# A hybrid diffusion layer on one core: later bank clearing, stepped head tails, earlier mLSTM decays, reordered output weights

## The chip, the cores and the metric

The kernel runs on one core of one Trainium2 chip. The metric is the device time of one execution in microseconds; lower is better. Three runs of the kernel before the change took 1374.45, 1374.62 and 1376.55 us, so its median is 1374.62 us. One further execution was taken with the hardware profiler; all rows of the trace below come from it.

The engines have short names in the profile: PE is TensorE (matrix products), PEld its weight loads, DVE is VectorE, ACT is ScalarE, POOL is GpSimd, and SP is the queue that issues nearly all DMAs. Every engine works its own queue strictly in order; between engines there are semaphores.

## The reference

One layer over 512 latent tokens (model width 1024) with 256 context tokens ahead of them, all in fp32:

```python
mod_x = (silu(c) @ w_ada + b_ada)            # six rows of 1024: shift, scale, gate, twice
hc = rms_norm(ctx, norm1_w) * (1 + mod_c[1]) + mod_c[0]
hx = rms_norm(x, norm1_w) * (1 + mod_x[1]) + mod_x[0]
_, states = token_mixer(hc, zero_states, False, ...)
x_mix, _ = token_mixer(hx, states, True, ...)
x = x + mod_x[2] * x_mix
hx = rms_norm(x, norm2_w) * (1 + mod_x[4]) + mod_x[3]
x = x + mod_x[5] * conv_ffn(hx, w_up, ffn_conv, w_down)   # 3x3 depthwise conv, silu gate, 2816 wide
return rms_norm(x, norm_out_w)
```

The token mixer has two branches, each run forward and backward over the tokens. The gated DeltaNet branch has 8 heads (keys and values 128 wide), the mLSTM branch has 4 (keys 128, values 256). Both are linear recurrences computed chunk by chunk: inside a chunk with a decay matrix, between chunks with a state. Each head's output is normalised and multiplied by a gate; the branches are projected back, merged by sigmoid gates and projected by `w_out`.

## The kernel before, in words

Tokens are taken in 6 chunks of 128 (2 of context, 4 latent). Large products are made in three passes of split operands (`mm3`, lines 117 to 122): a weight is cast to a high part on ScalarE (line 108) and its low part is a subtraction on VectorE or GpSimd (line 109). A raw weight lies in one of two to three raw buffers, its parts in as many split buffers; a load waits for a free one.

The stages follow each other: `streams` (norm, first modulation), `mixers` (12 heads), `merge` (branch projections and gates), `tail` (output projection, second norm, FFN, last norm).

In `mixers`, a loop over `s` runs the scan of head `s`: 0 to 7 are `gdn_scan`, 8 to 11 are `ml_scan`. A scan is a generator that yields after each short step. `drive` (line 1181) pulls it and, after each step, pulls side work at listed steps and a share of bulk work:

- the tail of the head before (`gdn_tail`, `ml_tail`), at steps 1, 4 and 6 (`TAIL`): square sums, a power on GpSimd, scaled copies out of PSUM, transposes;
- `merges(s + 1)` at steps 3, 4, 6, 8, 10, 12 and 13 (`MERGE`): it assembles the triangular inverses of the next head, and makes `qs`, the queries times a decay row that it loads by DMA;
- `ada_late`: the last four modulation rows by GpSimd products of `w_ada` tiles, some steps per scan from `s = 6` on; `ada_sum` adds them up in a PSUM tile `pad` on TensorE;
- as bulk, the preparation of head `s + 2` (`gdn_prep`, `ml_prep`): projections, keys, decay matrices `E` (loaded as rows by `decay_rows`, made by `weights`).

A scan adds its outputs into one PSUM bank `po`, of which there is one. `gdn_scan` clears it by a product with zeros (line 956) before its first step, and adds with `out` (line 961) from its third chunk step on. The bank is free when the tail of the head before has copied it out (line 1023).

The order in each queue is not the order of the lines. A planner lists all instructions, gives earlier lines priority, estimates durations, and issues on each engine what it takes to be ready. `queue_after(later, earlier)` ties an instruction behind another in this plan; `follow(ins, key)` ties it behind the latest anchor of that key: "t" for TensorE, "v" for VectorE, "s" for ScalarE, "d" for loads, "w" for casts, "p" for GpSimd. The result is a fixed queue per engine; on the chip an instruction whose input is late holds all behind it.

In `tail`, weights of `w_out` come in pairs of row blocks (`w_pair`, 512 KB each), four for each half of the output columns. The loads are serial (each tied behind the one before): the first half, a modulation row, `x` in four pieces, the second half from a separate pool, two modulation rows, then four weight tiles of `w_up` with a quarter of the filter rows `frow` behind each. The filter rows are transposed on TensorE into `fw` between the second half's products.

## Time and profile before

| | |
|---|---|
| median of 3 runs | 1374.62 us (1374.45 to 1376.55) |
| profiled execution, its time | 1377.58 us |
| its span, first to last instruction | 1375.8 us |
| mean granted TensorE clock | 0.983 |
| TensorE busy | 1310.2 us, 95% |
| VectorE busy | 890.2 us, 65% |
| ScalarE busy | 586.7 us, 43% |
| GpSimd busy | 541.4 us, 39% |
| DMA | 141.86 MB, mean 103 GB/s |

Each row of a timeline gives the start in us from the span's start, the duration in us, the engine, the line, the operation, `output<-inputs` by tile names, the shapes, and how many instructions the row holds. In square brackets stands how long the engine was idle just before, and which instruction or DMA ended that. A row of the view of waits gives who waited for whom, the sum in us, how often, and the longest. Matmuls are pipelined, so a busy TensorE is not TensorE at its peak: a matmul under a lowered clock counts as busy too. In time, the clearings of heads 1 to 7 run at about 238, 302, 359, 419, 475, 537 and 589 us, the mLSTM scans fill about 650 to 826, the merge 826 to 943, the output projection and second norm 943 to 1013, the FFN the rest.

### The profile page before, as it was taken

How to read it: one execution, taken by the hardware profiler on the slowest of the kernel's cores; microseconds unless marked ns; L12 is line 12 of the kernel's file. 1: busy time of each engine (PE TensorE's matmuls, PEld its weight loads, DVE VectorE, ACT ScalarE, POOL GpSimd, SP SyncE). 2: the span in 40 equal slices, each digit the busy share in tenths (PEclk: the TensorE clock that was granted, in tenths of full speed). 3: DMA queues.
4: the chain of work that ended last, by engine and by line, in shares of the span. 5: the costliest groups of instructions: out<-in, count | busy, mean ns of one | idle time of the engine just before them, and what ended most of it. 6: DMA issues, size and time to landing. Idle time of an engine off the chain costs nothing. (4 is left out here: it accounts for less than half of the span.)

```text
span 1375.8 us, 24216 instructions
## 1 busy us (share of the span) xinstructions
PE 1310.2 (95%) x9454; PEld 1103.0 (80%) x9454; DVE 890.2 (65%) x1809; ACT 586.7 (43%) x1283; POOL 541.4 (39%) x679
## 2 busy tenths in 40 slices
PE   6978999989899899999999999999899999999997
PEld 5867788878788788888888978888698888888876
DVE  5776686947568583524656466443769797997843
ACT  5555574645555554323333445221433333333322
POOL 4324222031231317475775670000246555455542
PEclk9989999999999999999999999999999999999999
DMA  9433233232232335343444432434623233333221
GB/s 284 123 103 81 76 90 106 67 76 76 53 90 62 81 69 139 99 123 92 129 120 112 116 100 69 138 107 168 175 77 107 92 92 92 105 95 90 94 92 62
DMA packets 233281, 141.86 MB, mean 103 GB/s; under 512 B 33025, under 2 KB 215566, under 8 KB 233166
## 3 DMA queue, kind: packets, MB, share of 16 engines
q1 hardware_dynamic: 231006, 140.09, 36.6%
q8 instruction: 74, 1.21, 0.4%
q10 hardware_dynamic: 2160, 0.23, 0.1%
q14 instruction: 41, 0.34, 0.1%
HBM read 134.47 MB, written 5.82 MB: 102 GB/s over the span
## 5 line engine op out<-in xcount | busy, mean ns | idle before, releaser
L1571 DVE SCALAR_TENSOR_TENSOR y<-pu,fw,y 128x441 f32<-128x441 f32 (+2 forms) x352 | 230.0, 691 | 43.1 <-ACT y L1562 37.2
L294 POOL TENSOR_TENSOR aw<-aw,sc 128x512 f32<-128x512 f32 x64 | 69.5, 1087 | 47.1 <-DMA aw<-in_w_ada_dram 47.1
L143 POOL TENSOR_TENSOR rs<-pw_t,mhalf 128x1 f32<-128x1 f32 x14 | 8.2, 583 | 167.5 <-DVE pw_t L142 167.5
L295 POOL TENSOR_TENSOR aw<-aw 128x256 f32<-128x256 f32 x64 | 54.4, 851 | 3.3
L143 POOL TENSOR_TENSOR kh<-pw_t,phalf 128x6 f32<-128x6 f32 x8 | 12.0, 1502 | 108.4 <-DVE pw_t L142 64.3
L884 POOL TENSOR_TENSOR qs<-qs,qT 128x512 f32<-128x512 f32 x16 | 25.0, 1565 | 69.3 <-DMA qs<-gd 58.6
L832 POOL MEMSET gx<- 96x16 f32 x8 | 1.0, 123 | 121.2 <-DMA gx<-scr 121.2
L986 ACT ACTIVATE v<-p,sc 128x128 f32<-128x128 f32 x80 | 25.5, 371 | 36.5 <-PE p L978 36.1
L974 DVE SCALAR_TENSOR_TENSOR X<-p,colA,vt 128x128 f32<-128x128 f32 x80 | 24.1, 339 | 25.1 <-PE p L970 24.8
L839 POOL TENSOR_TENSOR gx<-gx,iv_t 96x14 f32<-96x14 f32 (+6 forms) x112 | 36.6, 327 | 8.4
L1325 DVE SCALAR_TENSOR_TENSOR x<-x,py 128x512 f32<-128x512 f32 x16 | 11.0, 687 | 43.8 <-PE py L120 43.8
L1501 POOL TENSOR_TENSOR al<-y,ah 128x512 fp32r<-128x512 f32 x22 | 28.5, 1296 | 26.4 <-ACT ah L1500 26.4
L1562 ACT ACTIVATE y<-pu,fw 128x512 f32<-128x512 f32 x44 | 29.9, 682 | 17.7 <-PE pu L120 16.3
L990 PEld LDWEIGHTS p<-v,kt 128*128 128x128 f32 x160 | 22.6, 195 | 17.9 <-ACT v L986 16.7
L1133 DVE SCALAR_TENSOR_TENSOR C<-C,ge,mpc 128x257 f32<-128x257 f32 x32 | 15.3, 479 | 32.4 <-PE mpc L1129 32.0
L997 DVE SCALAR_TENSOR_TENSOR S<-S,ge,p 128x128 f32<-128x128 f32 x64 | 19.3, 340 | 26.2 <-PE p L990 25.8
L837 POOL TENSOR_TENSOR iv_t<-gx 96x14 f32<-96x14 f32 (+6 forms) x112 | 33.0, 295 | 8.0
L647 ACT ACTIVATE cv_t<-cv_y 128x512 f32<-128x512 f32 (+1 forms) x40 | 21.8, 545 | 33.6 <-DVE cv_y L646 32.7
L698 DVE SCALAR_TENSOR_TENSOR Eg<-Eg,colA,mask 128x128 f32<-128x128 f32 x96 | 31.5, 398 | 1.7 <-DMA Eg<-gd 1.7
L990 PE MATMUL p<-v,kt 128*128 128x128 f32 x160 | 27.9, 296 | 3.0 <-ACT v L986 3.0
L1003 ACT ACTIVATE v<-p,sc 128x128 f32<-128x128 f32 x64 | 22.9, 376 | 16.8 <-PE p L990 13.9
L1500 ACT CAST ah<-y 128x512 fp32r<-128x512 f32 x22 | 13.6, 619 | 38.0 <-DVE y L1499 37.8
(1222 smaller groups left out, 4593.4 us busy)
## 6 DMA issues: line engine op xcount, KB each, us to landing
aw<-in_w_ada_dram SPq DMA_DIRECT2D x64, 256.0 KB
uw<-in_w_ada_dram SPq DMA_DIRECT2D x16, 512.0 KB
Eg<-gd SPq DMA_DIRECT2D x16, 384.0 KB
qs<-gd SPq DMA_DIRECT2D x16, 256.0 KB
xn<-in_x_dram SPq DMA_DIRECT2D x4, 512.0 KB
Em<-r1d SPq DMA_DIRECT2D x8, 256.0 KB
mwo_0r<-in_w_in_dram SPq DMA_DIRECT2D x4, 512.0 KB
mwo_1r<-in_w_in_dram SPq DMA_DIRECT2D x4, 512.0 KB
```

The source lines that it names most:

```text
L294: self.follow(eng.tensor_tensor(w, w, self.sc[:, 4 * (j % 2) : 4 * (j % 2) + 4, 0:1].broadcast_to([P, 4, P]), ALU.mult))
L295: eng.tensor_tensor(w[:, 0:2, :], w[:, 0:2, :], w[:, 2:4, :], ALU.add)
L698: self.follow(nc.vector.scalar_tensor_tensor(E[:, c, :], E[:, c, :], self.colA[:, c, d, row : row + 1], self.mask[d], ALU.add, ALU.min), "v")
L837: eng.tensor_tensor(t, Bi[:, 0:j, j : j + 1].broadcast_to([8 * NB, j, n]), Bi[:, j : j + 1, j + 1 :].broadcast_to([8 * NB, j, n]), ALU.mult)
L839: g = eng.tensor_tensor(Bi[:, 0:j, j + 1 :], Bi[:, 0:j, j + 1 :], t, ALU.add)
L884: nc.gpsimd.tensor_tensor(x, x, qT, ALU.mult)
L974: self.anchor["v"] = nc.vector.scalar_tensor_tensor(X[d], p1[:, d, :], self.colA[:, c, 2 + d, h : h + 1], vt[:, c, :], ALU.mult, ALU.subtract)
L986: self.anchor["s"] = nc.scalar.activation(v3[d], p2[:, d, :], AF.Copy, scale=sc[d][:, 2 + j, c : c + 1])
L990: g = nc.tensor.matmul(p3[:, d, :], kt[:, c, :], v3[d], start=True, stop=True)
L1501: nc.gpsimd.tensor_tensor(al[:, j, :], ys[0], ah[:, j, :].bitcast(F32), ALU.subtract)
L1562: nc.scalar.activation(y, ps, AF.Copy, scale=tap(0, 0))
L1571: g = nc.vector.scalar_tensor_tensor(o, u3[:, r0 + dy : r1 + dy, c0 + dx : c1 + dx], tap(dy, dx), o, ALU.mult, ALU.add)
```

## The change

- The clearing of `po` moves from the start of a scan into `out`, just ahead of the first adding product, tied behind the scan's latest TensorE instruction.
- In `gdn_tail` the first seven heads yield between the power and the scaled copies, so the copies come at step 4 in place of step 1, tied behind ScalarE's latest scan instruction. The last head keeps its order.
- `qs` moves two stages later in `merges` (from the fourth stage to the sixth), and its multiplication on GpSimd is tied behind the latest power (`lastp`), that of a tail or of a head's key norm.
- Each tail's power becomes an anchor "q", behind which the products of `ada_late` are tied.
- In `ml_prep` the decay rows' loads come ahead of the key projection, and `weights` ahead of the output gate.
- The filter rows are loaded by one DMA at the start of `merge` and transposed there, into a tile `fw` that lives from there on.
- In `tail` the loads are reordered: all four pairs of the first half, two of the second, a modulation row and the first piece of `x`, the other two pairs, the rest of `x`, then two modulation rows; the fourth pair of the first half uses the separate pool, whose split buffers become five. In serial stretches, casts and subtractions are tied in order as well, and the FFN's second half becomes such a stretch.

```diff
--- before.py
+++ after.py
@@ -105,8 +105,12 @@
         lo = pool.tile(shape, F32R, tag="wlo", name=name + "l")
-        self.follow(nc.scalar.copy(hi, raw), "w")
+        c = nc.scalar.copy(hi, raw)
+        self.follow(c, "w")
         g = self.sub_eng.tensor_tensor(lo, raw, hi.bitcast(F32), ALU.subtract)
+        if self.serial:
+            self.follow(g, "l")
+            self.anchor["w"], self.anchor["l"] = c, g
         if self.late and self.sub_eng is nc.gpsimd:
@@ -140,7 +144,7 @@
         nc.vector.scalar_tensor_tensor(t, x, scale, (self.eps if bias else self.nil)[:, 0:n], ALU.mult, ALU.add)
-        nc.gpsimd.tensor_tensor(out, t, e[:, 0:n], ALU.pow)
+        return nc.gpsimd.tensor_tensor(out, t, e[:, 0:n], ALU.pow)
 
@@ -291,7 +295,9 @@
             nxt = load(j + 1) if j < 63 else None
-            self.follow(eng.tensor_tensor(w, w, self.sc[:, 4 * (j % 2) : 4 * (j % 2) + 4, 0:1].broadcast_to([P, 4, P]), ALU.mult))
+            g = eng.tensor_tensor(w, w, self.sc[:, 4 * (j % 2) : 4 * (j % 2) + 4, 0:1].broadcast_to([P, 4, P]), ALU.mult)
+            self.follow(g)
+            self.follow(g, "q")
             eng.tensor_tensor(w[:, 0:2, :], w[:, 0:2, :], w[:, 2:4, :], ALU.add)
@@ -733,7 +739,7 @@
         kh = small.tile([P, NCH], F32, tag="kh", name=f"kh{h}")
-        self.rpow(kh, ssk, 0.25, 0.0, self.phalf)
+        self.lastp = self.rpow(kh, ssk, 0.25, 0.0, self.phalf)
         yield 0.65
@@ -876,14 +882,6 @@
         yield
-
-        qs = []
-        for d in range(2):
-            x = hold.tile([P, NT], F32, tag="qs", name=f"qs{h}_{d}", bufs=4)
-            nc.sync.dma_start(x, self.gd[1, h, d : d + 1, NCTX:].broadcast_to([P, NT]))
-            nc.gpsimd.tensor_tensor(x, x, qT, ALU.mult)
-            qs.append(x)
-        self.qs[h] = qs
         DD = [(Bt[d], Dm_[:, d]) for d in range(2)]
@@ -915,6 +913,14 @@
         yield
+
+        qs = []
+        for d in range(2):
+            x = hold.tile([P, NT], F32, tag="qs", name=f"qs{h}_{d}", bufs=4)
+            nc.sync.dma_start(x, self.gd[1, h, d : d + 1, NCTX:].broadcast_to([P, NT]))
+            self.queue_after(nc.gpsimd.tensor_tensor(x, x, qT, ALU.mult), self.lastp)
+            qs.append(x)
+        self.qs[h] = qs
 
@@ -949,16 +955,16 @@
         qs = self.qs[h]
-        po = self.pt([P, XC, P], "po", f"po{h}")
-        self.po[h] = po
         S = [None, None]
         self.left = 4 * XC
-        nc.tensor.matmul(po, self.zero, self.zero.unsqueeze(1).broadcast_to([P, XC, P]), start=True, stop=False)
         order = [list(range(NCH)), list(range(CC - 1, -1, -1)) + list(range(NCH - 1, CC - 1, -1))]
...
         def out(x, a, b):
+            if self.left == 4 * XC:
+                self.po[h] = self.pt([P, XC, P], "po", f"po{h}")
+                self.follow(nc.tensor.matmul(self.po[h], self.zero, self.zero.unsqueeze(1).broadcast_to([P, XC, P]), start=True, stop=False))
             self.left -= 1
-            nc.tensor.matmul(po[:, x, :], a, b, start=False, stop=self.left == 0)
+            nc.tensor.matmul(self.po[h][:, x, :], a, b, start=False, stop=self.left == 0)
 
@@ -1017,12 +1023,15 @@
         nc.vector.scalar_tensor_tensor(f, ss, 1.0 / P, ssq, ALU.mult, ALU.add)
-        nc.gpsimd.tensor_tensor(f, f, self.mhalf[:, 0:XC], ALU.pow)
+        self.anchor["q"] = self.lastp = nc.gpsimd.tensor_tensor(f, f, self.mhalf[:, 0:XC], ALU.pow)
+        if h < GH - 1:
+            yield 0.0
         o = self.hold.tile([P, XC, P], F32, tag="o", name=f"o{h}", bufs=2)
         for c in range(XC):
-            nc.scalar.activation(o[:, c, :], po[:, c, :], AF.Copy, scale=f[:, c : c + 1])
+            self.follow(nc.scalar.activation(o[:, c, :], po[:, c, :], AF.Copy, scale=f[:, c : c + 1]), "s" if h < GH - 1 else None)
         yield 0.0
-        yield 0.0
+        if h == GH - 1:
+            yield 0.0
         ps = self.pt([P, 512], "prep", f"pot{h}")
@@ -1046,6 +1055,7 @@
         wk = self.w_cols(w, O_MK + P * h, f"mwk{h}")
+        E = [self.decay_rows(d, 8 + h, list(range(CC, NCH)), f"m{h}_{d}") for d in range(2)]
         kT = hold.tile([P, NALL], F32, tag="kT", name=f"mkT{h}", bufs=3)
@@ -1056,7 +1066,8 @@
         nc.scalar.activation(qT, p, AF.Copy, scale=P ** -0.5)
-        E = [self.decay_rows(d, 8 + h, list(range(CC, NCH)), f"m{h}_{d}") for d in range(2)]
+        for d in range(2):
+            self.weights(E[d], d, 8 + h, range(CC, NCH))
         og = []
@@ -1075,7 +1086,6 @@
         for d in range(2):
-            self.weights(E[d], d, 8 + h, range(CC, NCH))
             a = hold.tile([P, XC, P], F32, tag=f"at{d}", name=f"mp{h}_{d}", bufs=3)
@@ -1160,7 +1170,7 @@
         f = small.tile([P, XC], F32, tag="fo", name=f"mfo{h}")
-        self.rpow(f, ss, 1.0 / MDV, EPS, self.mhalf)
+        self.anchor["q"] = self.rpow(f, ss, 1.0 / MDV, EPS, self.mhalf)
         yield 0.0
@@ -1304,6 +1314,9 @@
                 pass
+            frow = self.flat(I["ffn_conv"]).rearrange("(c r p) -> r c p", r=99, p=P)
+            fr = self.hold.tile([99, 4, P], F32, tag="aw", name="frow", bufs=3)
+            nc.sync.dma_start(fr, frow)
             free = [self.slots[:, j, :] for j in range(self.nkept, 8)]
@@ -1325,6 +1338,8 @@
                 nc.vector.tensor_tensor(t[0], t[0], t[1], ALU.add)
+                if n < 4:
+                    self.cols_of(self.fw[:, 99 * n : 99 * n + 99], fr[:, n, :], 99)
                 nc.scalar.copy(self.mh[:, n, :], t[0])
@@ -1348,7 +1363,7 @@
             self.ps = es.enter_context(tc.tile_pool(name="ps", bufs=1, space=PSUM))
-            mg_es, l1 = ExitStack(), ExitStack()
+            mg_es, fw_es, l1 = ExitStack(), ExitStack(), ExitStack()
             with ExitStack() as e1:
@@ -1370,11 +1385,13 @@
                 self.dump("oTm", self.oTm)
+                self.fw = fw_es.enter_context(tc.tile_pool(name="fwp", bufs=1, side="right")).tile([P, 9 * 44], F32, tag="fw", name="fw")
                 self.mgt = mgt = mg_es.enter_context(tc.tile_pool(name="mgt", bufs=1, side="right"))
...
             self.tail(mg_es)
+            fw_es.close()
             l1.close()
@@ -1391,33 +1408,29 @@
             nw = lp.tile([P, D], F32, tag="nw", name="nw")
-            self.fw = lp.tile([P, 9 * 44], F32, tag="fw", name="fw")
             h2 = tuple(lp.tile([P, KC, NT], F32R, tag=f"h2{i}", name=f"h2{i}") for i in range(2))
...
                 m2, B2, A2 = rows = [ad1.tile([P, D], F32, tag=f"mr{i}", name=f"mr{i}") for i in range(3)]
-                x = (e2.enter_context(tc.tile_pool(name="wraw3", bufs=2)), e2.enter_context(tc.tile_pool(name="wsp3", bufs=4)))
+                x = (e2.enter_context(tc.tile_pool(name="wraw3", bufs=2)), e2.enter_context(tc.tile_pool(name="wsp3", bufs=5)))
                 w = I["w_out"][0]
...
                 self.wi, self.serial, self.anchor = 3, True, {}
-                wt = [self.w_pair(w, 0, b0) for b0 in range(0, KC, 2)]
+                wt = [self.w_pair(w, 0, 2 * i, x if i == 3 else None) for i in range(4)]
+                w1 = [self.w_pair(w, 1, 2 * i, x) for i in range(2)]
+                self.mod_row(0, m2)
+                self.load(x1[:, 0, :], I["x"][0, :P, :])
+                w1 += [self.w_pair(w, 1, 4, x), self.w_pair(w, 1, 6, x)]
+                for c in range(1, XC):
+                    self.load(x1[:, c, :], I["x"][0, c * P : c * P + P, :])
+                self.mod_row(2, A2)
+                self.mod_row(1, B2)
                 for b0 in range(0, KC, 2):
...
                         self.tok_mm(ps[c], wt[b0 // 2], self.mh, self.ml, b0, c, KC)
-                self.mod_row(0, m2)
-                for c in range(XC):
-                    self.load(x1[:, c, :], I["x"][0, c * P : c * P + P, :])
-                wt = [self.w_pair(w, 1, b0, x) for b0 in range(0, KC, 2)]
-                self.mod_row(2, A2)
-                self.mod_row(1, B2)
-                wu = []
-                frow = self.flat(I["ffn_conv"]).rearrange("(r p) -> r p", p=P)
-                fr = []
-                for b in (0, NFF, 1, NFF + 1):
-                    wu.append(self.w_cols(I["w_up"][0], P * b, f"wu{b}"))
-                    fr.append(ad1.tile([99, P], F32, tag="frow", name=f"frow{len(fr)}", bufs=4))
-                    self.load(fr[-1], frow[99 * len(fr) - 99 : 99 * len(fr), :])
+                self.wi = 3
+                wu = [self.w_cols(I["w_up"][0], P * b, f"wu{b}") for b in (0, NFF, 1, NFF + 1)]
                 self.serial = False
@@ -1431,8 +1444,7 @@
                     for i in range(4):
-                        self.tok_mm(p, wt[i], self.mh, self.ml, 2 * i, c, KC)
-                    self.cols_of(self.fw[:, 99 * c : 99 * c + 99], fr[c], 99, self.bank(5, f"ps_fw{c}"))
+                        self.tok_mm(p, w1[i], self.mh, self.ml, 2 * i, c, KC)
                     residual(c, 1, p)
@@ -1522,6 +1534,7 @@
             last = NFF - 6
+            self.serial = True
             for b0 in range(0, last, 2):
```

## The prediction

> **What bounds the kernel now.** I read the page first, then TensorE's waits by line, then the granted clock in short stretches, and last the engines' timelines around the longest waits. The first line of the page's part 1 says where the time is:
>
> ```profile
> PE 1310.2 (95%) x9454; PEld 1103.0 (80%) x9454; DVE 890.2 (65%) x1809; ACT 586.7 (43%) x1283; POOL 541.4 (39%) x679
> ```
>
> TensorE (PE) is busy for 95% of the span, and the change adds and removes no matmul. So it can only earn what TensorE loses to waiting, and it earns that one for one as long as no other engine takes its place. The view of waits, TensorE alone (us in total, times, longest), has these rows for the places that the change touches; the row of `mp` stands for comparison:
>
> ```profile
> PE po L956 <- ACT o L1023: 11.2, 4, 3.3
> ...
> PE p L990 <- ACT v L986: 3.0, 5, 0.6
> ...
> PE pv L119 <- ACT va L1099: 2.5, 1, 2.5
> PE mpqk L1075 <- DVE mkt L1071: 2.4, 1, 2.4
> ...
> PE mp L1137 <- ACT mn L1141: 2.2, 2, 1.6
> ...
> PE pt L1464 <- DVE h L1468: 2.1, 1, 2.1
> PE ps_fw L216 <- DMA frow<-in_ffn_conv_dram: 2.0, 2, 1.8
> ...
> PE pd L119 <- POOL wt_8l L109: 1.3, 1, 1.3
> ...
> PE po L119 <- DVE rs_t L1426: 0.7, 1, 0.7
> ```
>
> The largest single wait of the kernel is the clearing of a scan's bank (L956), which waits for the copies out of that bank (L1023). The touched rows add up to 11.2 + 3.0 + 2.5 + 2.4 + 2.1 + 2.0 + 1.3 + 0.7 = 25.2 us.
>
> A wait costs more than its own length here. The view of stretches (length, busy time of PE, PEld, DVE, ACT, POOL, then the granted TensorE clock, DMA share, GB/s) right behind five of these waits, with one undisturbed stretch between them:
>
> ```profile
> 302.00:307.00 5.00, 4.39 (x14) 3.48 (x14) 1.46 (x4) 3.53 (x8) 0.00 (x0) 0.66 0.00 0
> 360.50:364.50 4.00, 4.00 (x13) 3.27 (x14) 1.40 (x4) 2.80 (x7) 0.00 (x0) 0.57 0.02 4
> 476.50:480.50 4.00, 4.00 (x13) 3.28 (x14) 1.46 (x5) 2.86 (x7) 0.00 (x0) 0.57 0.00 0
> 480.50:530.00 49.50, 49.50 (x603) 42.57 (x602) 33.68 (x85) 27.22 (x84) 12.80 (x37) 1.00 0.35 80
> 633.00:638.00 5.00, 5.00 (x33) 5.00 (x32) 3.33 (x7) 0.52 (x2) 0.07 (x1) 0.66 0.53 152
> 995.50:999.50 4.00, 3.88 (x19) 3.32 (x19) 3.48 (x5) 2.16 (x4) 2.42 (x3) 0.57 0.01 2
> ```
>
> In each the clock falls for a few microseconds; the loss is 5 x (1 - 0.66) = 1.7 us, or 4 x (1 - 0.57) = 1.7 us. The reader is to see that a wait of 2 to 3 us is followed by 1.7 us more, lost in matmuls that look busy.
>
> Now the boundary between two scans, around 352 to 367 us: the timelines of POOL, VectorE (DVE), ScalarE (ACT) and TensorE in this order.
>
> ```profile
> 355.16 2.02 POOL L884 TENSOR_TENSOR qs<-qs,qT 128x512 f32<-128x512 f32 x1 [4.38 <-DMA qs<-gd]
> 357.14 1.01 POOL L1020 TENSOR_TENSOR fo<-fo,mhalf 128x4 f32<-128x4 f32 x1
> ```
>
> ```profile
> 351.83 0.16 DVE L1019 SCALAR_TENSOR_TENSOR fo<-sso,ssq 128x4 f32<-128x4 f32 x1 [1.50 <-ACT junk L1017]
> ```
>
> ```profile
> 358.18 1.14 ACT L1023 ACTIVATE o<-po,fo 128x128 f32<-128x128 f32 x4 [6.08 <-POOL fo L1020]
> 359.20 0.86 ACT L699 ACTIVATE Eg<-Eg 128x768 f32<-128x768 f32 x1
> 359.93 0.64 ACT L986 ACTIVATE v<-p,sc 128x128 f32<-128x128 f32 x2
> ```
>
> ```profile
> 359.37 0.38 PE L956 MATMUL po<-zero 128*128 128x512 bf16 x1 [3.29 <-ACT o L1023]
> 360.36 0.95 PE L990 MATMUL p<-v,kt 128*128 128x128 f32 x4 [0.61 <-ACT v L986]
> 360.97 1.20 PE L119 MATMUL px_k<-hx,wk5h 128*128 128x512 f32 x2
> ...
> 366.21 0.39 PE L961 MATMUL po<-S,qs 128*128 128x128 f32 x2
> ```
>
> The factor `fo` is ready for its power on POOL at 351.99 (351.83 + 0.16), but POOL's queue has a multiplication of `qs` ahead of it, which waits for its DMA until 355.16 and then runs 2.02 us. The power ends at 358.15, so ScalarE, whose next instruction is the copy, stands for 6.08 us; the clearing stands behind the copies, the new scan's `v` (L986) stands behind them too, and L990 waits for that. The two rows of TensorE, 3.29 and 0.61, are one cause.
>
> **The change part by part.**
>
> *Clearing, tail in steps, later qs.* Three edits act on this one place. The clearing moves to just ahead of the scan's first adding product, the row at 366.21, 6.8 us behind where it stood (366.21 - 359.37). The copies move to the fourth step of the next scan, behind its `v`, so `v` no longer stands behind them. And `qs` goes behind the latest power on POOL. With POOL free at 351.99 the power ends at 353.0 and the copies (1.14) could end at 354.2, well ahead of the clearing. Removed: 11.2 us, three of the five L990 waits (3 x 0.6 = 1.8), and the three slow stretches at 302, 360.5 and 476.5 (3 x 1.7 = 5.1): 18.1 us. The upper end is 19.3 with all five L990 waits; the lower is 6, if the copies at their new place still end late in some scans. Three closed waits have the same rows behind them, so I take 17.
>
> The two `qs` multiplications themselves are unchanged; what is late next could be their users. The tightest is the first scan, whose `qs` is now queued behind a power of head 2; its row, and the first product that reads `qs`:
>
> ```profile
> 176.60 1.45 POOL L143 TENSOR_TENSOR kh<-pw_t,phalf 128x6 f32<-128x6 f32 x1 [4.07 <-DVE pw_t L142]
> 189.34 0.38 PE L961 MATMUL po<-S,qs 128*128 128x128 f32 x2
> ```
>
> Behind 178.05 come two multiplications of at most 2.02: 182.1, with 7.2 us of cover before 189.34. Cost 0; without cover, TensorE would wait in the first scan for what exceeds 7.2.
>
> The adaLN products (L294) now also queue behind each tail's power. POOL stands still if that power waits for VectorE; behind it come only sums for `pad`. In the mLSTM stretch POOL has room:
>
> ```profile
> 650.00:826.00 176.00, 170.42 (x969) 148.34 (x967) 99.02 (x211) 65.91 (x137) 126.84 (x148) 1.00 0.43 113
> ```
>
> 49 us are free there (176 - 126.84), 12 per scan of four, so I cost it at 0; without that room each later sum would hold TensorE at L311.
>
> *mLSTM decays sooner.* Rows of VectorE at two heads:
>
> ```profile
> 626.56 5.59 DVE L698 SCALAR_TENSOR_TENSOR Em<-Em,colA,mask 128x128 f32<-128x128 f32 x8
> 632.08 1.01 DVE L1071 COPY mkt<-ps_tm_mk 128x256 f32<-128x256 f32 x2
> ```
>
> ```profile
> 705.98 0.61 DVE L698 SCALAR_TENSOR_TENSOR Em<-Em,colA,mask 128x128 f32<-128x128 f32 x2 [7.46 <-DMA Em<-r1d]
> ```
>
> At 626.56 eight decay instructions stand ahead of the copy that frees a bank for `mpqk`: the 2.4 us wait, plus the slow stretch at 633. The change traces them ahead of the output gate's matmuls, so they should be done before: 2.4 + 1.7 = 4.1, I take 4. At 705.98 VectorE waits 7.46 us for the decay row's DMA, ScalarE's exponential behind it holds the copy `va`, and TensorE waits 2.5 us for that. The load is traced ahead of the query weights' load now, but its buffer comes free no sooner; I take half, 1.3. Together 5.3, between 0 (the same order comes out) and 6.6.
>
> *Output weights, filter rows.* Here ScalarE, VectorE and the DMA queue around 967 to 980:
>
> ```profile
> 977.33 1.04 ACT L108 CAST wu0h<-wu0r 128x1024 fp32r<-128x1024 f32 x1 [4.69 <-DMA wu0r<-in_w_up_dram]
> ```
>
> ```profile
> 978.40 1.23 DVE L109 TENSOR_TENSOR wu0l<-wu0r,wu0h 128x1024 fp32r<-128x1024 f32 x1 [4.51 <-ACT wu0h L108]
> 979.55 0.68 DVE L1426 TENSOR_TENSOR rs_t<-po,mr 128x512 f32<-128x512 f32 x1
> ```
>
> ```profile
> 967.83 0.37 SPq L98 DMA_DIRECT2D wt_6r<-in_w_out_dram  x1
> 968.25 0.93 SPq L98 DMA_DIRECT2D mr<-mrd  x2
> 969.22 0.43 SPq L98 DMA_DIRECT2D wu0r<-in_w_up_dram  x1
> ```
>
> The wait for `frow` (2.0) goes, since those rows are loaded in the merge. But under it lies a second one: `rs_t` stands behind the split of `wu0`, which waits for its DMA; with `frow` alone gone, TensorE would meet that wait at nearly the same time. What brings the second forward is the new order of loads: the last pair of output weights is issued at 967.83 only because a raw buffer has to come free, and everything behind it waits too. With the fourth pair of the first half in the other pool and five split buffers there, the queue holds less. I take 2.2 of 2.0 + 0.7. The norm's transposes (pt, 2.1 + 1.7 = 3.8) wait for a VectorE queue that carries these splits; I take a third, 1.3. Together 3.5, between -1.2 (one split, 1.23, lands ahead of a residual) and 6.5. The filter's four transposes and copies move into the merge at the same number: 0.
>
> *Serial order of the last weights.* One row of POOL, whose split of chunk 8 came after those of 10 and 12:
>
> ```profile
> 1327.00 2.81 POOL L109 TENSOR_TENSOR wt_8l<-wt_8r,wt_8h 128x1024 fp32r<-128x1024 f32 x1
> ```
>
> In order, chunk 8 is split a whole 2.8 us sooner, and TensorE's 1.3 goes: I take 1.2, between -1.2 and 1.3, because loads in order also wait for each other's buffers.
>
> *What comes back.* The order of all queues is planned anew, and a plan leaves some waits of its own. I allow two of the size of `pt` with its slow stretch, 2 x 3.8 = 7.6. Sum: 17 + 5.3 + 3.5 + 1.2 - 7.6 = 19.4 us. The profiled execution took 1377.58 us (span 1375.8), so 1358.2 in its terms; it stands 3.0 above the median of the runs, 1374.62, from which 19.4 leaves **1355.2 us**.
>
> *One rule against the trace.* The rows above show half-clock stretches behind waits of 2.1 to 3.3 us. The Trainium skill, "TensorE: Matmul & The Clock Gate" (Part 1: The HAM clock gate), says that the gate closes after an idle window of about 3.4 us and that pauses longer than this are the ones to avoid. By it none of these waits would touch the clock. The trace disagrees: 2.4 us were enough at 633, though the length of a stretch, about 3.4 us at half rate, fits its window.
>
> **The rivals.**
> 1. *Half comes back.* The scan's chain has other links on ScalarE (the row at 359.20, 0.86, stands ahead of `v`), so closing one wait opens a smaller one. For it: the L990 rows in five scans, not four. Against it: those links have run by 355 once ScalarE no longer stands. Half of 18.1 returns: 1364.2.
> 2. *The clock does not follow.* The slow stretches stay although the waits close, because smaller gaps bring them. For it: the 2.5 us wait of `pv` does not stand in front of one of the five. Against it: 49.5 us at 1.00 without a wait. Without the clock's part of my terms (5.1 + 1.7 + 0.6 = 7.4): 1362.6. This is also where the skill's rule would end.
> 3. *No new waits.* All upper ends, 19.3 + 6.6 + 6.5 + 1.3 = 33.7: 1340.9.
> 4. *The plan puts things back.* Trace order is only a priority; the planner issues what it thinks ready. The waits move and the sum is zero: 1374.6. Against it: the ties to the power and to `v` are hard.
> 5. *Slower: the copies come too late at their new place.* If on ScalarE the copies, now tied behind `v` and competing with casts and exponentials, end behind the first adding product, each of seven clearings waits as the worst did, 3.29 + 0.61 + 1.7 = 5.6, so 39 us in place of 18.1; with the other terms (5.3 + 3.5 + 1.2 - 7.6 = 2.4) that is 18.7 slower, 1393.3. It decides at the point where the copies end later than the row at 366.21 stands now; by the rows there are 12 us between (366.21 - 354.2).
>
> **How the numbers follow.** Chances: forecast 0.55 (its own range 1347 to 1362), half back 0.18, clock 0.07, no new waits 0.07, no change 0.05, slower 0.08. The range 1345 to 1370 leaves out the most of rivals 3, 4 and 5, about 0.2. 0.2% is 2.7 us and about what a measurement of this kernel tells from no change: faster 0.55 + 0.18 + 0.07 + 0.07 = 0.87, less 0.01 for cases that shrink to nothing, 0.86; within 0.05; slower 0.09.
>
> **What would show it.** L956 no longer among TensorE's waits, the `fo` power directly behind its VectorE row with no `qs` ahead, fewer stretches below 0.7 between 300 and 640; decays ahead of the `mkt` copy; `frow` gone from 977 and `wu0` cast before it; chunk 8 split before 10. Wrong would be: L956 waiting for L1023 at its new place, first products waiting for `qs`, TensorE idle at L311, or a new wait of more than 4 us where the page of before has none.

## The result, and the profile after

The changed kernel takes 1342.2 us (median of six runs, 1339.6 to 1343.6) against 1374.5 for the kernel before (six runs, 1369.0 to 1376.6): a ratio of 0.9769, 95% interval 0.9749 to 0.9789, or 32 us less. Forecast were 19.4 us less. One run of the kernel before, taken beside the last two experiments below, took 1445.4 us at a granted clock of 0.844, and every difference leaves it out. The profiled execution took 1340.27 us, 2 below its median, where that of before stood 3 above its own; so the two profiles differ by 37.3 us, 5 more than the kernels do.

The first line of part 1 of the changed kernel's page, and TensorE's waits by line (us in total, times, longest):

```profile
PE 1293.4 (97%) x9454; PEld 1096.0 (82%) x9454; DVE 895.0 (67%) x1809; ACT 585.1 (44%) x1283; POOL 534.9 (40%) x679
```

```profile
PE pqk L772 <- DVE gx L767: 3.0, 2, 2.5
PE pad L317 <- POOL as L307: 2.6, 4, 1.2
...
PE po L967 <- ACT v L1009: 2.2, 4, 0.6
...
PE pv L123 <- ACT va L1109: 1.4, 1, 1.4
PE pt L1476 <- DVE h L1480: 1.4, 1, 1.4
```

Gone are the clearing (11.2), `mpqk` (2.4), `ps_fw` (2.0) and `wt_8l` (1.3). New among the longest is `pqk`, 2.5 us in one place. TensorE's gaps over 0.15 us sum to 57.4 us before and 37.2 after; the stretches at half clock last 47.7 us before and 23.9 after, and that difference is worth 11.9 us at half rate. Together these are 32.1 of the 37.3 us; the rest lies in TensorE's busy time (1310.2 to 1293.4 us) and is not explained here.

The same boundary between two scans as in the prediction, in the changed kernel: VectorE, GpSimd, ScalarE, TensorE.

```profile
340.22 0.17 DVE L1025 SCALAR_TENSOR_TENSOR fo<-sso,ssq 128x4 f32<-128x4 f32 x1 [1.51 <-ACT junk L1023]
```

```profile
340.47 1.01 POOL L1026 TENSOR_TENSOR fo<-fo,mhalf 128x4 f32<-128x4 f32 x1 [1.81 <-DVE fo L1025]
```

```profile
343.65 0.61 ACT L992 ACTIVATE v<-p,sc 128x128 f32<-128x128 f32 x2
...
344.85 1.14 ACT L1031 ACTIVATE o<-po,fo 128x128 f32<-128x128 f32 x4
```

```profile
356.64 0.38 PE L965 MATMUL po<-zero 128*128 128x512 bf16 x1
356.86 0.39 PE L967 MATMUL po<-S,qs 128*128 128x128 f32 x2
```

The power follows its VectorE row at once, with no `qs` ahead. `v` goes ahead of the copies, the copies end at 345.99, and the clearing comes 10.7 us later (356.64 - 345.99) without waiting.

Where the time went is read from the first start of every tile on TensorE, changed kernel less kernel before: -12 us by 161 us of the span of before, back to -8 by 193, -25 by 549, -30 by 655, -31 by 943, -35 by 1024, -37 at the end. Two of these are not in the prediction's sum: the 12 us of the prelude (the first 160 us or so, in which the first heads are prepared), and the 4 us that come back behind it.

### The profile page after: what moved, and what is told of

It reads as the page before. It is cut to its first block, busy times and chain, and to the rows that moved or that the text cites. A ratio compares the mean times of both kernels' runs of the same rounds, so it can differ in the third digit from the quotient of the medians.

```text
span 1338.5 us, 24202 instructions
## 1 busy us (share of the span) xinstructions
PE 1293.4 (97%) x9454; PEld 1096.0 (82%) x9454; DVE 895.0 (67%) x1809; ACT 585.1 (44%) x1283; POOL 534.9 (40%) x679
## 4 chain that ended last, share of the span: by engine, by line
PE 71%; DVE 7%; ACT 5%; DMA 2%; issue 1%; POOL 1%; SPq 0%; POOLq 0%; ACTq 0%; DVEq 0%
PE pu L123 12%; PE pd L123 6%; PE pu L124 6%; PE py L123 4%; PE px_g L123 4%; PE pv L123 3%; PE pd L124 3%; PE py L124 2%; PE px_mo L123 2%; PE px_g L124 2%; PE px_z L123 2%; PE po L967 2%; PE p L984 2%; PE pv L124 1%; PE p L976 1%
## 5 line engine op out<-in xcount | busy, mean ns | idle before, releaser
L843 POOL TENSOR_TENSOR iv_t<-gx 96x14 f32<-96x14 f32 (+6 forms) x112 | 35.9, 320 | 8.1
L1151 ACT ACTIVATE mn<-mp,colA 128x257 f32<-128x257 f32 x32 | 15.2, 475 | 32.3 <-PE mp L1147 30.3
L967 PE MATMUL po<-v,at 128*128 128x128 f32 x128 | 26.0, 285 | 2.2 <-ACT v L1009 2.2
L1009 ACT ACTIVATE v<-p,sc 128x128 f32<-128x128 f32 x64 | 22.9, 375 | 11.7 <-PE p L996 8.8
L1525 DVE TENSOR_TENSOR fd_t<-pd,m 128x512 f32<-128x512 f32 (+1 forms) x10 | 6.2, 634 | 32.1 <-PE pd L124 32.1
L704 DVE SCALAR_TENSOR_TENSOR Eg<-Eg,colA,mask 128x128 f32<-128x128 f32 x96 | 26.5, 348 | 1.6 <-DMA Eg<-gd 1.6
L976 PE MATMUL p<-S,kT 128*128 128x128 f32 x160 | 27.1, 287 | 0.4 <-DVE S L1001 0.4
```

What stands on the lines that cost most here:

```text
L843: eng.tensor_tensor(t, Bi[:, 0:j, j : j + 1].broadcast_to([8 * NB, j, n]), Bi[:, j : j + 1, j + 1 :].broadcast_to([8 * NB, j, n]), ALU.mult)
L967: nc.tensor.matmul(self.po[h][:, x, :], a, b, start=False, stop=self.left == 0)
L976: g = nc.tensor.matmul(p1[:, d, :], kT[:, c * P : c * P + P], S[d], start=True, stop=True)
```

## The experiments

Differences are between medians, each against the runs of the kernel before on the same chip. The intervals are those of the ratio of the times.

| run | median us | against before | ratio, 95% interval |
|---|---|---|---|
| qs_only | 1356.45 | -17.5 | 0.9841 to 0.9889 |
| clear_tail_only | 1354.89 | -19.1 | 0.9833 to 0.9885 |
| clear_only | 1363.09 | -11.2 | 0.9906 to 0.9944 |
| decays_only | 1370.04 | -3.9 | 0.9952 to 0.9990 |
| outputs_only | 1366.76 | -7.7 | 0.9923 to 0.9966 |
| after_again | 1341.54 | -32.7 | 0.9731 to 0.9779 |
| after_qs_early | 1341.95 | -32.0 | 0.9745 to 0.9799 |
| after_no_ada_tie | 1341.26 | -33.0 | 0.9741 to 0.9786 |
| after_kh_late | 1340.17 | -34.2 | 0.9730 to 0.9775 |
| after_qs_vector | 1340.01 | -34.4 | 0.9729 to 0.9776 |
| after_qs_pieces | 1335.31 | -38.9 | 0.9698 to 0.9739 |
| before_qs_pieces | 1369.34 | -4.3 | 0.9943 to 0.9982 |
| after_early_pieces | 1342.58 | -31.0 | 0.9762 to 0.9815 |

**The scan boundary: three edits, one at a time.** First `qs` alone:

```diff
-            nc.gpsimd.tensor_tensor(x, x, qT, ALU.mult)          # fourth stage of merges
+            self.queue_after(nc.gpsimd.tensor_tensor(x, x, qT, ALU.mult), self.lastp)   # sixth stage
```

> The kernel before with one edit: qs goes two stages later in merges, and its multiplication on GpSimd is tied behind the latest power. The clearing stays at the scan's start and the tail keeps its order. Theory A (relief): two gains. In the prelude, four qs multiplications no longer run beside VectorE's decay instructions (1.38 us each there, 0.34 without), which gave 8 us; at the scan boundaries the fo power no longer stands behind qs, so the copies end about 354.2 and the clearing at 356.1 finds the bank free: 14 to 17 us. Sum -22 to -25 us, about 1351. Theory B (the prelude's gain is an accident of the new order or of the run): the boundaries alone, -14 to -17 us, about 1359, and the head's decay rows at 90 and 127 us keep 3.7 and 5.3 us. Theory C (the later clearing is what closed the waits): -8 us at most, and L956 keeps most of its 11.2 us.

The load of `qs` moves with the product. Measured: -17.5 us. Its POOL, ScalarE and TensorE at the second boundary:

```profile
343.31 1.01 POOL L1020 TENSOR_TENSOR fo<-fo,mhalf 128x4 f32<-128x4 f32 x1 [1.31 <-DVE fo L1019]
```

```profile
344.35 1.14 ACT L1023 ACTIVATE o<-po,fo 128x128 f32<-128x128 f32 x4 [1.02 <-POOL fo L1020]
```

```profile
347.15 0.39 PE L956 MATMUL po<-zero 128*128 128x512 bf16 x1
```

With the power no longer behind `qs`, the clearing finds its bank free at the old place. That refutes theory C, and it confirms the reading that the wait came from GpSimd's queue; whether the later stage or the tie does it was not separated. The sum is near theory B's, but the prelude shows theory A: its decays take 1.67, 1.66 and 3.23 us. What that earns, a new wait `pqk` of 2.5 us takes back in part. Then the other pair of edits, with `qs` untouched:

```diff
+            if self.left == 4 * XC:      # in out(): clear ahead of the first adding product
+                self.po[h] = ...
+                self.follow(nc.tensor.matmul(self.po[h], self.zero, ...))
...
+        if h < GH - 1:
+            yield 0.0                    # in gdn_tail: copies a step later, behind "s"
```

> The kernel before with two edits: the clearing moves to the first adding product and the tail's copies come a step later behind the scan's ScalarE work; qs stays where it was, without a tie. Theory A: the power still waits behind qs till 358.2, but the clearing has 6.8 us of cover and v no longer stands behind the copies: -16 to -18 us, about 1357, with the prelude unchanged (waits pc_k 2.7 and px_z 3.1 us stay). Theory B: the same at the boundaries and the same in the prelude as in the changed kernel, -24 us. Theory C (ScalarE stands for the power all the same, only later): -5 to -9 us, and the first adding product waits for L1023.

Measured: -19.1 us, and no wait for the clearing. So each of the two remedies closes the boundary alone. The clearing by itself, without the tail's steps:

```diff
-        self.po[h] = po      # and the clearing product, at the scan's start
+            if self.left == 4 * XC:      # in out(), as above; gdn_tail as in the kernel before
```

> The kernel before with one edit: the clearing moves to the first adding product; the tail's copies stay at step 1 and qs stays where it was. Theory A (the cover counts: 6.8 us behind the old place): the waits at L956 go with their slow stretches, -14 to -19 us, as clearing and tail together gave (-19). Theory R (the queue counts): v still stands behind the copies on ScalarE, and these behind the power, till 359.9 in the second scan; TensorE meets it at L990, which stands right behind the old place: L956's 11.2 us turn into L990's, 0 to -5 us, 1370 to 1374. Then it is the tail's later copies, or the later qs, that close the wait.

Measured: -11.2 us, between the two. The view of waits of this run:

```profile
PE p L990 <- ACT v L986: 10.2, 6, 3.9
```

Before, L956 and L990 took 11.2 + 3.0 = 14.2 us; now L990 alone takes 10.2. Most of the wait has moved to the next instruction that stands behind the late copies on ScalarE, as theory R says, and the cover won 4 us. Two slow stretches of the three at the boundaries stayed (301 and 356 us). The rest of the 11 lies elsewhere, 3 us of it behind 590 us, where nothing was changed: there `pv` waits 0.6 us in place of 2.5, and there is one slow stretch fewer (1.7 us; last section).

**What the later `qs` adds.** The changed kernel with `qs` back at its old stage and without the tie:

```diff
-            self.queue_after(nc.gpsimd.tensor_tensor(x, x, qT, ALU.mult), self.lastp)   # sixth stage
+            nc.gpsimd.tensor_tensor(x, x, qT, ALU.mult)          # fourth stage of merges
```

> The changed kernel with one edit undone: qs is back at its old stage in merges, without the tie to the latest power. Theory A: the four slow decay instructions of the prelude come back, the boundaries stay closed by the later clearing: 7 to 9 us over the changed kernel, about 1350. Theory B: within 2 us of the changed kernel, 1342. If qs is what closed the boundaries: 20 us or more over it, 1362.

Measured: 1341.95, the same as the changed kernel. So with the boundary closed by the clearing and the tail, moving `qs` is worth nothing in sum, and the 7 to 9 us of theory A are not there. But the traces are not the same. In the prelude of the kernel before these are decay rows of VectorE, and GpSimd beside the second of them:

```profile
88.31 1.67 DVE L698 SCALAR_TENSOR_TENSOR Eg<-Eg,colA,mask 128x128 f32<-128x128 f32 x6 [1.71 <-DMA Eg<-gd]
90.31 3.73 DVE L698 SCALAR_TENSOR_TENSOR Eg<-Eg,colA,mask 128x128 f32<-128x128 f32 x6
...
127.53 5.31 DVE L698 SCALAR_TENSOR_TENSOR Eg<-Eg,colA,mask 128x128 f32<-128x128 f32 x12
```

```profile
90.61 2.75 POOL L884 TENSOR_TENSOR qs<-qs,qT 128x512 f32<-128x512 f32 x2 [16.04 <-DMA qs<-gd]
```

Six decays take 1.67 us alone and 3.73 beside two products of `qs`. The changed kernel, where no `qs` runs there, and TensorE behind the second group in both kernels:

```profile
86.47 1.66 DVE L704 SCALAR_TENSOR_TENSOR Eg<-Eg,colA,mask 128x128 f32<-128x128 f32 x6
121.53 3.24 DVE L704 SCALAR_TENSOR_TENSOR Eg<-Eg,colA,mask 128x128 f32<-128x128 f32 x12
```

```profile
133.37 1.19 PE L119 MATMUL px_z<-hx,wz1h 128*128 128x512 f32 x2 [3.10 <-DVE ssk L732]
```

```profile
125.31 0.70 PE L123 MATMUL px_z<-hx,wz1h 128*128 128x512 f32 x2 [1.04 <-DVE ssk L738]
```

The `qs` products of heads 0 and 1 now run together, behind the key power of head 2. There they meet that head's small scalings `sc` (L749, L751), and TensorE pays:

```profile
166.28 5.33 POOL L921 TENSOR_TENSOR qs<-qs,qT 128x512 f32<-128x512 f32 x4
```

```profile
166.29 1.30 DVE L749 TENSOR_SCALAR sc<-sc 128x6 f32<-128x6 f32 x1
...
167.59 1.26 DVE L749 TENSOR_SCALAR sc<-sc 128x6 f32<-128x6 f32 x1
...
169.70 0.71 DVE L751 TENSOR_SCALAR sc<-sc 128x6 f32<-128x6 f32 x1
...
170.59 1.05 DVE L751 TENSOR_SCALAR sc<-sc 128x6 f32<-128x6 f32 x1
```

```profile
171.94 1.16 PE L772 MATMUL pqk<-qT,kT 128*128 128x128 f32 x8 [2.47 <-DVE gx L767]
```

Without `qs` beside them (in after_qs_early) these scalings take 0.16 to 0.17 us each. Over all traces of the layer, the six whose prelude has no `qs` reach the place that lies at 161 us in the profiled execution of before 6.5 to 12.2 us sooner, on average 8.8; seven others with `qs` at its old place, in whole or cut products, reach it 1.6 to 5.9 sooner, on average 3.8. So some 5 us are the edit, and nearly 4 us were this one execution of the kernel before. In the changed kernel about 4 are gone again behind `pqk`: its wait of 2.5 and the slow stretch behind that (1.7).

**The disputed cost by itself.** A kernel that leaves the layer out. Each kind of VectorE instruction runs once alone and once together with `mul(8)`:

```python
v.scalar_tensor_tensor(E[i % 4], E[i % 4], col[:, 0:1], mask, ALU.add, ALU.min)   # 128x128, a decay
v.scalar_tensor_tensor(y[i % 2], y[i % 2], col[:, 0:1], h, ALU.add, ALU.min)      # 128x512
v.tensor_copy(y[i % 2], h)                                                        # from SBUF
v.tensor_copy(y[i % 2], ps)                                                       # from PSUM
g.tensor_tensor(q[i % 2], q[i % 2], h, ALU.mult)                                  # mul: 128x512, as qs
```

> Not the layer: a kernel that leaves all of it out and runs four kinds of VectorE instruction alone and beside eight GpSimd multiplications of 128x512 (the shape of qs): the decay instruction (scalar_tensor_tensor 128x128, two inputs from SBUF), the same on 128x512, a copy of 128x512 from SBUF, a copy of 128x512 from PSUM. Theory A: alone the decay instruction takes 0.27 to 0.35 us; beside GpSimd each takes about what one GpSimd product takes, 1.3 us; the copy from SBUF is held likewise; the copy from PSUM is not. Theory B (no contention): all equal to their time alone.

The view of one source line, in five windows of the probe (times in ns: least, median, most; then first and last start in us) gives the decay instruction, first alone, then beside GpSimd; then a copy from SBUF, alone and beside GpSimd; then a copy from PSUM beside GpSimd:

```profile
L36 DVE SCALAR_TENSOR_TENSOR E<-E,col,mask x24: 336/338/374, 7.7 to 13.7; 128x128 f32<-128x128 f32 x24
L36 DVE SCALAR_TENSOR_TENSOR E<-E,col,mask x9: 374/1345/1346, 26.5 to 35.6; 128x128 f32<-128x128 f32 x9
L44 DVE COPY y<-h x17: 416/417/419, 69.6 to 75.0; 128x512 f32<-128x512 f32 x17
L44 DVE COPY y<-h x10: 419/1479/1486, 78.6 to 89.1; 128x512 f32<-128x512 f32 x10
L48 DVE COPY y<-pb x14: 677/678/682, 105.7 to 113.4; 128x512 f32<-128x512 f32 x14
```

338 ns become 1345, one VectorE instruction for each GpSimd product of about 1305 ns (1262 alone). The copy from PSUM is untouched. Theory A holds in all three.

**Four ways to take the collision away.** The key power, and `qs` behind it, meant to come behind `sc`:

```diff
-        self.lastp = self.rpow(kh, ssk, 0.25, 0.0, self.phalf)      # ahead of the sc loop
+        self.lastp = self.rpow(kh, ssk, 0.25, 0.0, self.phalf)      # behind it
+        self.queue_after(self.lastp, last)                          # last: the last sc product
```

> The changed kernel with one edit: the key norm's power kh (and with it qs, which is tied behind it) comes behind the eight small sc products on VectorE, ahead of which it stood. Theory A (a GpSimd product on 128x512 holds VectorE's instruction from SBUF till it ends): in head 2 the sc products no longer take 1.30, 1.26, 0.71 and 1.05 us in place of 0.17, so the wait pqk at 169.5 (2.47) and the slow stretch behind it (1.7) go: -3 to -4 us, 1338.5, and the prelude keeps its gain. Theory B (pqk waits for something else, or the prelude's gain is a run's accident): within 1 us of the changed kernel, 1342. Later heads give nothing, since their pqk did not wait.

Measured: 1340.17, with `pqk` still at 2.47. The planned order hardly changed: GpSimd still started `qs` at 167.20 and the first held `sc` took 1.31 us at 167.21. The power, tied in the plan behind the last `sc` product (171.52), ran at 165.91 on the chip. So the edit did not separate the two, and this run decides nothing. The four early products on VectorE:

```diff
+            if h < 2:
+                nc.vector.tensor_tensor(x, x, qT, ALU.mult)
+            else:
```

> The changed kernel with one edit: the four qs multiplications of heads 0 and 1 run on VectorE, without the tie; those of the other heads stay on GpSimd. Theory A: no GpSimd product on 128x512 is left in the prelude, VectorE pays 4 x 0.7 = 2.8 us, of which some lies ahead of decays and sc: -1 to -4 us, 1338 to 1341, sc products at 0.17 us, no pqk wait. Theory B: 0 to +2 us, 1342 to 1344, the work on VectorE costs what the wait did.

Measured: 1340.01, inside theory A's range but too near to the changed kernel (1342.2, and 1336.1 to 1342.6 in its other runs) to tell. The `pqk` wait of head 2 is gone. The price is on VectorE:

```profile
PE pc_k L123 <- DVE cv_y L652: 5.5, 2, 3.1
```

Two waits of 3.1 and 2.4 us, at 95 and 132 us, took the place of one. Then the same products on GpSimd at the same place, each cut in four:

```diff
+            for i in range(4):
+                y = x[:, 128 * i : 128 * i + 128]
+                self.queue_after(nc.gpsimd.tensor_tensor(y, y, qT[:, 128 * i : 128 * i + 128], ALU.mult), self.lastp)
```

> The changed kernel with one edit: each qs multiplication of 128x512 on GpSimd is cut into four of 128x128, same place, same tie, same order on VectorE. Theory A (a VectorE instruction with its operands in SBUF waits until the GpSimd instruction that runs has ended): the sc products of head 2 take at most 0.5 us each in place of 1.30, 1.26, 0.71 and 1.05, VectorE is 2 to 3 us sooner, the wait pqk at 169.5 falls from 2.47 to under 0.5 and its slow stretch goes: -2 to -4 us from the changed kernel, 1338 to 1340. Theory B (the two engines share the bandwidth, so that GpSimd's whole work counts, not the length of one instruction): the sc products lose as much in sum, the wait stays, within 1 us of the changed kernel, 1342.

Measured: 1335.31 (1334.6 to 1336.9), 6.2 us under the changed kernel on the same chip and more than theory A gave. GpSimd and VectorE at head 2:

```profile
169.95 7.08 POOL L923 TENSOR_TENSOR qs<-qs,qT 128x128 f32<-128x128 f32 x16
```

```profile
169.97 0.47 DVE L749 TENSOR_SCALAR sc<-sc 128x6 f32<-128x6 f32 x1
...
170.43 0.44 DVE L749 TENSOR_SCALAR sc<-sc 128x6 f32<-128x6 f32 x1
...
171.72 0.32 DVE L751 TENSOR_SCALAR sc<-sc 128x6 f32<-128x6 f32 x1
...
172.22 0.24 DVE L751 TENSOR_SCALAR sc<-sc 128x6 f32<-128x6 f32 x1
```

GpSimd works longer (7.08 us for 5.33), and yet the four scalings take 1.5 us in place of 4.3. So the length of one GpSimd instruction decides what a lone VectorE instruction loses; theory B falls. Gone are `pqk` (2.47), the same wait at head 3 (0.5, and 0.7 at `ps_gt`), and all four `po` waits (0.5 each; after_qs_early has none either, so they come with whole products at the new place). This version beats both kernels.

Last, cut products at the old place, in both kernels:

```diff
+            for i in range(4):
+                y = x[:, P * i : P * i + P]
+                nc.gpsimd.tensor_tensor(y, y, qT[:, P * i : P * i + P], ALU.mult)     # fourth stage, no tie
```

> The kernel before with one edit: each qs multiplication is cut into four of 128x128 at its old place, without a tie. Theory A (length of one GpSimd instruction): in the prelude six decays take 3 us in place of 3.73 (1.66 without qs) and twelve 4.3 in place of 5.31, so the waits pc_k (2.7) and px_z (3.1) shrink by 0.7 to 1 each and perhaps a slow stretch goes: -1.5 to -5 us, 1369 to 1372.5; the boundaries keep L956. Theory P (place in the queue): the waits pc_k and px_z stay as they are, 1374 within 1.5 us, or they grow, since four pieces take 1.8 us where one took 1.3 and kh's power stands behind them.

> The changed kernel with qs at its old stage, without the tie, and in pieces of 128x128. Theory A: against the changed kernel with qs at its old stage in whole products (1342) the prelude's two waits shrink as above: -1.5 to -5 us, 1337 to 1340.5; not better than pieces at the new place (1335.3), where the decays of the prelude meet no product at all. Theory P: 1342 within 1.5 us.

Measured: -4.3 us in the kernel before, and 1342.58 in the changed kernel, no gain there. The waits of the prelude shrink, three of four by less than the 0.7 to 1 us of theory A: `px_z` from 3.1 to 2.7 in both kernels, `pc_k` from 2.7 to 2.3 in the kernel before and from 2.5 to 1.7 in the changed one. The second group of decays and the pieces beside it, in before_qs_pieces:

```profile
123.03 4.86 DVE L698 SCALAR_TENSOR_TENSOR Eg<-Eg,colA,mask 128x128 f32<-128x128 f32 x12
```

```profile
123.19 3.76 POOL L886 TENSOR_TENSOR qs<-qs,qT 128x128 f32<-128x128 f32 x8 [7.46 <-DVE qT L648]
```

Twelve take 4.86 us; they took 5.31 beside whole products and 3.24 with none. Single instructions show why: of these twelve the two whole products held two, at 1.38 us each, and the eight pieces hold eight, at 0.54 each (0.34 alone). Where many such instructions stand in a row, each piece holds the next one, and the loss falls only from 2.07 to 1.62 us. Pieces help single instructions, as `sc`; decays have to be kept clear of GpSimd. A part of the 4.3 us is at the boundaries, against the expectation:

```profile
PE po L958 <- ACT o L1025: 7.4, 4, 3.4
```

The clearing waits 7.4 us in all, where it waited 11.2 in the kernel before and 9.3 and 9.5 in outputs_only and decays_only, which leave this place alone. That is 2 to 4 us less, in two of the four waits; the others grew. Why those two shrink is left open.

**The other parts.** Decays of the mLSTM alone, and all edits from the merge on alone (the filter rows, the order of loads, the fifth split buffer, casts and subtractions in order, the serial second half of the FFN):

```diff
+        E = [self.decay_rows(d, 8 + h, ...) for d in range(2)]        # decays_only: ahead of the key projection
...
+            self.weights(E[d], d, 8 + h, range(CC, NCH))              # ahead of the output gate
```

```diff
+            nc.sync.dma_start(fr, frow)                               # outputs_only: in merge
...
+                wt = [self.w_pair(w, 0, 2 * i, x if i == 3 else None) for i in range(4)]
...
+            self.serial = True                                        # ahead of the FFN's second half
```

> The kernel before with one edit: the mLSTM heads' decay rows are loaded ahead of the key projection and made ahead of the output gate. Forecast's term: -5.3 us, 1369, the waits mpqk (2.4) and pv (2.5, half) gone with one slow stretch at 634. Rival: the planner puts the decay instructions at the same place and nothing changes (1374 within 1.5 us); or they displace other VectorE work of the last delta scans, 0 to +3 us.

> The kernel before with the edits from the merge on: filter rows loaded and transposed in the merge, the reordered loads of output weights, five split buffers, casts and subtractions in order, the FFN's second half serial. Forecast's terms: 3.5 + 1.2 = -4.7 us, about 1369.5; frow (2.0) and rs_t (0.7) gone, pt still there. Reading of the two traces: 3.7 us between 943 and 1024 and 1.4 at the end, -5. What is left of the difference between the changed kernel and the kernel before after the single parts (19 for clearing and tail, 4 for the decays) is 9: if the parts simply add, -9 us, 1365.

Measured: -3.9 and -7.7 us. With the decays moved, `mpqk` is gone and `pv` still waits 2.2. In outputs_only `ps_fw` and `wt_8l` are gone, `pt` waits 1.4 where it waited 2.1, and the wait for `rs_t` is still there (0.9 at `pu`, 0.7 at `po` before). By the first starts it gains 5 us between 943 and 1024 and 1.7 behind 1302. Its edits were not taken apart. The changed kernel without the tie of the adaLN products, and the changed kernel once more:

```diff
-            self.follow(g, "q")
```

> The changed kernel without the tie of the adaLN products behind each tail's power. Forecast's term: 0, within 1 us of the changed kernel, 1342. Rival: the tie (or the earlier scans) made pad wait 2.6 us where it waited 0.7 before; without it pad is back under 1 us: -2 us, 1340. If the tie protects the power from standing behind adaLN products: +2 to +6 us, and copies or first products wait in the last delta scans.

> The changed kernel itself, for the spread between two profiled executions of one program and as the neighbour of the other three on this chip. 1342.2 within 1.5 us; the waits pqk (2.5), pt (1.4), pad (2.6) and the four of po (0.6 each) come again at the same places; slow stretches that no wait stands in front of (70.8, 77.7) may move by several us.

Measured: 1341.26 and 1341.54, no difference that the spread would show: the tie costs nothing. `pad` waits 2.6 and 1.5 us in the two profiles with the tie and 0.4 without, but without it `mp` waits up to 1.6 in place of 0.8 and `pqk` up to 3.4 in place of 2.5.

## Why the prediction was off, step by step

- **Clearing, tail, later `qs` (17).** Clearing and tail alone gave 19.1. The reading of the rows was right: the power behind `qs`, the copies behind the power, the clearing and `v` behind the copies. What it missed is that the three edits are two full remedies for one wait. Half coming back, its first rival, would have left about 9 (interval of the measured part 15.8 to 22.9).
- **`qs` moved, at 0.** Wrong on both sides, though right in sum. The step asked only who reads `qs`, and there it held: no product waits for it. Its sizes were off without harm: four products stand behind that power, not two, and the kernel before has one of 3.05 us (at 296.65), over the "at most 2.02"; the first reader comes at 186.99, behind their end at 171.61. It did not ask what GpSimd's products do to VectorE while they run. That gave some 5 us in the prelude and took some 4 at `pqk` and 1.2 at head 3.
- **adaLN tie, at 0.** Right: 1341.26 without, 1341.54 with.
- **mLSTM decays (5.3).** 3.9 measured, interval 1.4 to 6.6. In the changed kernel the eight decays run at 581.57 and the `mkt` copy at 602.06, as foretold; only the half taken for `pv` did not come by this edit alone (2.2 us in place of 2.5).
- **Output weights (3.5) and serial order (1.2).** 7.7 together, interval 4.7 to 10.6. `wu0` is cast at 939.84 in place of 977.33, chunk 8 is split before 10 and 12. The 2.2 taken for `frow` and `rs_t` brought 2.0 - 0.2, as `rs_t` is still waited for. The term that was too small is the norm's transposes (1.3): they wait 1.4 in place of 2.1, and in outputs_only the slow stretch at 995.6 went whole, together 2.4 (the changed kernel has one there, at 961.7).
- **What comes back (-7.6).** This is the step that failed most. The three parts measured alone sum to 19.1 + 3.9 + 7.7 = 30.7, about 5 either way by their intervals, and the whole is 32.2: a loss of 7.6 on top of the parts would have left 23. New waits did come, and of the size allowed: `pqk` 2.5 with its slow stretch 1.7, `pad` 1.9 more (0.8 in after_again), `po` 2.2. But the `po` waits stand in for the 3.0 of L990 (0.4 now), which the sum had counted as gone by 1.8, and the prelude's relief, which the sum had at 0, pays for `pqk`; in after_qs_early, where neither of these two stands, 32.0 us are gained all the same. The allowance counted losses alone, with no row behind it, and left out that a new plan can gain as well.

So of the 12.8 us missed, 7.6 are the allowance, 3.7 the sizes (30.7 - 27.0), and 1.5 are what the whole has over its parts; the last two lie within the intervals. The rival without new waits (1340.9) came closest in number, but not in kind, and the rival of no change lies far outside the interval. The rival of the late copies falls by 10.7 us of distance. The rival in which the clock does not follow falls at the boundaries, where no slow stretch is left between 300 and 640.

## What to carry to other kernels

When a queue is relieved by moving one of its instructions, look at what the moved instruction will run beside, not only at who reads it: here a product on GpSimd held decays, small scalings and copies on VectorE whose operands lay in SBUF. If it cannot be kept away from a chain that TensorE waits for, short pieces take more GpSimd time in all (7.08 us in place of 5.33) but hold a single instruction for less; for a long row of such instructions they won little. And measure the parts alone before allowing for a loss that no row shows.

## What the hardware showed that was not expected

**The lock between GpSimd and VectorE.** In the probe the engines take turns, instruction by instruction: 1345 ns for a decay of 338, and with a scalar_tensor_tensor of 128x512 (739 ns alone) both take about 1.7 us. The Trainium skill, "SBUF — State Buffer" (Who interferes with whom), says the same: the two engines share a pair of ports by an exclusive lock held for a whole instruction, and a VectorE instruction with at most one input from SBUF, outside the fast two-port modes, does not meet it. The trace agrees, with 678 ns for the copy from PSUM in either case. By that rule the prelude's cost could have been read before the change.

**The clock looks at fixed windows.** The prediction added 1.7 us to each wait of 2 to 3 us. In 15 traces of the layer all stretches at half clock begin on one grid of 3.41 us per trace, so the place of a wait on that grid should decide. Counted over the windows at full clock, from a trace's first slow stretch to its end: where TensorE was idle for 1.92 us or more of a window, the next was at half clock in 49 of 49 cases; between 1.2 and 1.92 us in 28 of 97; below that in 1 of 5323. (The two bounds are read off these same counts.) The views below show a wait of 2.9 us that fell mostly in one window (2.3 us of it), in outputs_only, and one of 2.6 that was cut by a window's edge (1.5 and 1.1), in clear_only: each time the stretch of the wait and the one behind it (the last three columns are the granted clock, the DMA share and GB/s):

```profile
625.70:628.60 2.90, 0.06 (x1) 0.00 (x0) 2.90 (x6) 1.10 (x5) 2.67 (x5) 1.00 0.15 45
629.70:633.10 3.40, 3.40 (x19) 3.40 (x18) 2.75 (x6) 0.37 (x1) 0.00 (x0) 0.51 0.48 123
```

```profile
620.50:623.00 2.50, 0.00 (x0) 0.00 (x0) 2.50 (x5) 0.98 (x4) 2.27 (x4) 1.00 0.00 0
623.10:626.60 3.50, 3.50 (x30) 3.50 (x31) 3.50 (x7) 0.60 (x2) 0.00 (x0) 1.00 0.21 49
```

The same `mpqk` wait brings the half clock in one run and not in the other. It also explains what the prediction's second rival leaned on, the 2.5 us wait of `pv` in the kernel before with no slow stretch behind it: an edge cut it into 1.5 and 1.0. And it is one reason why profiles of one program differ in the prelude: the changed kernel's two are 4.2 us apart by the place at 161 us, and 1.7 of that is the clock (10.2 and 13.7 us at half rate). The Trainium skill, "TensorE: Matmul & The Clock Gate" (Part 1: The HAM clock gate), has the free-running window of 3413 ns, which these traces confirm; that an idle window is needed they do not, since 1.9 us of one were enough.
